# Early gathered steps beside the query product, and low weight halves on GpSimd in one stretch of a decoder-layer kernel

## The chip, the cores and the metric

The kernel runs on one core of a Trainium2 chip. The metric is the device time of one execution in microseconds (us), and less is better. The time of the kernel before is the median of three runs; beside them one execution was profiled, and every row shown here is of that one.

## The reference

The kernel computes one hybrid decoder layer on 512 tokens with 2048 channels, in float32:

```
x = x + concat[conv_group(xn), swa_group(xn)] @ w_out
x = x + peer(rms_norm(x))

peer: qh   = xt @ peer_w_q                    # 8 heads, two halves of 128
      sub  = qh . peer_sub_keys               # 128 scores per half
      v1, i1 = top_k(sub[0], 16); v2, i2 = top_k(sub[1], 16)
      cand = v1[:, None] + v2[None, :]        # best 16 of the sums
      experts = e1 * 128 + e2; gates = softmax(vals)
      h = xt . peer_u[experts];  a = gelu(h) * gates
      y = sum over 8 heads x 16 of a * peer_v[experts]
```

Each token thus picks 128 of 16384 experts, each one row of peer_u and one row of peer_v.

## The kernel before

The work goes in this order: the input product with convolution and attention, the two halves of the output product, the query product (`wq`) with the choice of experts, and then the experts themselves. All weights stream as **units** of 128x1024 float32 (512 KB). `stream` (L124 to L137) loads a unit into `w_raw` by SyncE's queue, ScalarE copies it rounded into `w_hi` (L135) and VectorE subtracts to get the rest, `w_lo` (L136); `w_hi` and `w_lo` have three buffers each, `w_raw` four from the second half of the output product on. Each product is three matmuls (high by high, low by high, high by low). Units 0 to 51 are the input product, 52 to 83 the output product, 84 to 115 the query product, and from 116 on come the experts.

The experts are computed in two ways. For the first 352 tokens they are **dense**: every expert is computed for every token. The sweep (`expert_tile`, L914) multiplies `peer_u`, the fold (`fold_group`, L960) multiplies `peer_v` by the gated results. One expert tile or one fold step is two units, 48 matmuls of 352 columns, and is called a **tick** here (`step`, L908): ticks 1 to 72 are sweep, 73 to 184 take turns of 8 sweep and 8 fold ticks, 185 to 256 are fold. The query product is 8 heads of 4 units, 24 matmuls of 512 columns each; after a head its queries go through `qhh` and `qhl` (L171, L172) into the score matmuls of `head_sub` (L676 to L678).

The other 160 tokens are **gathered**: `gather_step` (L829) fetches one row of `peer_u` or `peer_v` per partition by an indirect DMA that GpSimd issues (L821, 1 MB into `grow`, two buffers). VectorE then does one instruction over 128x2048: a product with its sum for `peer_u` (L837), a multiply and add into `yrow` for `peer_v` (L851). There are 320 steps: 128 + 32 over `un`, then 128 + 32 over `vn`. At the very end `yrow` goes through four products (`yo`, L1029), four copies (L1030) and one store (L1031).

When a gathered step is written into the program is set by the tick: from tick 11 (`START` = 10) to tick 247 (`END`) the steps are spread evenly, and the gather is put behind the first matmul of the tick (`add_manual_dep`, an order for the planner and no wait on the chip). The planner decides the order of each engine's queue beforehand; each engine then works through its queue in order.

```
if tick[0] > START:
    gather_until(int((tick[0] - START) * STEPS / (END - START)) + 1, first)
```

The choice of experts is VectorE work (`top16`, `gates`, `decode`) put into two waiting lists by `head_topk` (L760). `pump` hands some of it out after each unit, by written costs; its last piece for a head, `head_idx` (L755), writes 16 columns of `idx`, the list of rows to gather for that head.

Of the kernel before, what the change touches and what calls it, by code (L numbers as in the profile page):

```python
# [9 lines left out]
FT = mybir.dt.float32  # L10
FR = mybir.dt.float32r
# [3 lines left out]
OP = mybir.AluOpType  # L15
AX = mybir.AxisListType

T, D = 512, 2048
KC = D // 128
NT = T // 128  # L20
TD = 352
# [4 lines left out]
GT = 16  # L26
AHEAD = 9
START = 10
END = 247.0
PUMP = 5.4  # L30
CONV_K = 31
HD, NQ = 64, 16
NK, PH, TOPK = 128, 8, 16
# [26 lines left out]
def hymba_layer(ctx: ExitStack, tc: tile.TileContext, xT, pos, par, row, wi, wo, wq, sk, ut, un, vt, vn,  # L60
                out_t, out_r, dbg=None):
    nc = tc.nc
# [9 lines left out]
    dram = ctx.enter_context(tc.tile_pool(name="dram", bufs=1, space=bass.MemoryType.DRAM))  # L72
    mm = ctx.enter_context(tc.tile_pool(name="mm", bufs=4, space=PS))
# [7 lines left out]
    def later(cost, fn, *a, low=False):  # L81
        queues[low].append((cost, fn, a))
# [3 lines left out]
    def pump(us):  # L86
        credit[0] = min(credit[0] + us, us)
        for q in queues:
            while q and credit[0] > 0:
                cost, fn, a = q.popleft()  # L90
                fn(*a)
                credit[0] -= cost

    def drain(low=True):
        for q in queues[:1 + low]:
            while q:
                _, fn, a = q.popleft()
                fn(*a)
# [26 lines left out]
    def stream(upto):  # L125
        while nxt[0] < min(upto, len(specs)):
            i = nxt[0]
            nxt[0] += 1
            raw = raws[-1][0].tile([128, 1024], FT, name="w_raw", bufs=raws[-1][1])
            with tc.high_priority(offset=400 if i >= 4 else 0):  # L130
                nc.sync.dma_start(raw, specs[i])
            hi = ring.tile([128, 1024], FR, name="w_hi", bufs=3)
            lo = ring.tile([128, 1024], FR, name="w_lo", bufs=3)
            with tc.high_priority(offset=400):
                nc.scalar.activation(hi, raw, AF.Copy)  # L135
                nc.vector.tensor_tensor(lo, raw, hi.bitcast(FT), op=OP.subtract)  # L136
            units[i] = (hi, lo)  # L137

    def unit(ahead=1):
        i = nxt[1]  # L140
        nxt[1] += 1
        stream(i + 1 + ahead)
        return units.pop(i)
# [26 lines left out]
    def split(hi, lo, src):  # L170
        nc.scalar.activation(hi, src, AF.Copy)  # L171
        nc.vector.tensor_tensor(lo, src, hi.bitcast(FT), op=OP.subtract)  # L172
# [444 lines left out]
    nh = np_.tile([128, KC, T], FR, name="nh")  # L617
    nl = np_.tile([128, KC, T], FR, name="nl")
# [37 lines left out]
    es_q = ExitStack()  # L656
    wqp = es_q.enter_context(tc.tile_pool(name="wqp", bufs=1, side="right"))
# [10 lines left out]
    def head_sub(h, qh, ql, kh, kl):  # L668
        vv = kp.tile([128, NT, 2, 16], FT, name="vv", bufs=8)
        ii = kp.tile([128, NT, 2, 16], U32, name="ii", bufs=8)  # L670
        hs[h] = {"vv": vv, "ii": ii}
        hs[h]["sub"] = []
        st = kp.tile([128, 2, T], FT, name="subT", bufs=1)
        for p in range(2):
            ps = aux_bank([128, T], "subT")
            nc.tensor.matmul(ps, kh[:, p], qh[:, p], start=True, stop=False)  # L676
            nc.tensor.matmul(ps, kl[:, p], qh[:, p], start=False, stop=False)
            nc.tensor.matmul(ps, kh[:, p], ql[:, p], start=False, stop=True)  # L678
            nc.scalar.activation(st[:, p], ps, AF.Copy)
        for tp in range(2):  # L680
            ps = aux_bank([128, 2, 2, 128], "sub")
            for t in range(2):
                for p in range(2):
                    ts = slice((2 * tp + t) * 128, (2 * tp + t) * 128 + 128)
                    nc.tensor.transpose(ps[:, t, p], st[:, p, ts], ident)
            sub = kp.tile([128, 2, 2, 128], FT, name="sub", bufs=4)
            nc.scalar.activation(sub, ps, AF.Copy)
            hs[h]["sub"].append(sub)
# [66 lines left out]
    def head_idx(h):  # L755
        s = slice(h * 16, h * 16 + 16)
        nc.vector.scalar_tensor_tensor(idx[:, s], E1[:, 3, h], 128.0, E2[:, 3, h], op0=OP.mult, op1=OP.add)
        nc.vector.tensor_copy(GA3[:, s], GA[:, 3, h])

    def head_topk(h):  # L760
        for t in range(NT):
            later(2.1, first16, h, t)
        later(0.8, cands, h, low=True)
        for t in range(NT):
            later(1.0, second16, h, t, low=True)
        later(2.5, gates, h, low=True)
        later(3.3, decode, h, 0, low=True)
        later(3.3, decode, h, 1, low=True)
        later(0.2, head_idx, h, low=True)

    def lane_lists():
# [6 lines left out]
        for l in range(LANES):  # L778
            nc.scalar.dma_start(idxb[l * NB:l * NB + NB], ib[ps_, l * SB:l * SB + SB])
            nc.scalar.dma_start(GB3[l * NB:l * NB + NB], ga[:, l * SB:l * SB + SB])  # L780

    for h in range(PH):
        kr = wqp.tile([128, 2, 128], FT, name="kr", bufs=2)
        nc.sync.dma_start(kr, sk[h])
        kh = wqp.tile([128, 2, 128], FR, name="kh", bufs=2)
        kl = wqp.tile([128, 2, 128], FR, name="kl", bufs=2)
        split(kh, kl, kr)
        banks = [mm.tile([128, T], FT, name="mm") for _ in range(2)]
        for u in range(4):
            hi, lo = unit()  # L790
            for kc in range(4):
                k = 4 * u + kc
                for j in range(2):
                    s = slice(kc * 256 + j * 128, kc * 256 + j * 128 + 128)
                    nc.tensor.matmul(banks[j], hi[:, s], nh[:, k], start=k == 0, stop=False)  # L795
                    nc.tensor.matmul(banks[j], hi[:, s], nl[:, k], start=False, stop=False)  # L796
                    nc.tensor.matmul(banks[j], lo[:, s], nh[:, k], start=False, stop=k == KC - 1)  # L797
            pump(3.6)
        qh = wqp.tile([128, 2, T], FR, name="qhh", bufs=1)
        ql = wqp.tile([128, 2, T], FR, name="qhl", bufs=1)  # L800
        for j in range(2):
            split(qh[:, j], ql[:, j], banks[j])
        head_sub(h, qh, ql, kh, kl)
        head_topk(h)
    drain(low=False)
    es_q.close()

    later(0.5, lane_lists, low=True)
    H = [dram.tile([128, 4, TD], FT, name=f"H{i}") for i in range(32)]
    NCH = TD // GT  # L810
    G = dram.tile([16, 128, NCH, 8, GT], FT, name="G")

    pu = ctx.enter_context(tc.tile_pool(name="pu", bufs=1))
    h3 = gat.tile([128, 128 + SB], FT, name="h3")
# [1 line left out]
    STEPS = 2 * (128 + SB)  # L816
# [34 lines left out]
            nc.vector.scalar_tensor_tensor(y, g, h3[:, k:k + 1], y, op0=OP.mult, op1=OP.add)  # L851

    done = [0]

    def gather_until(n, after):
        while done[0] < min(n, STEPS):
            gather_step(done[0], after)
            done[0] += 1

    es_g = ExitStack()  # L860
    gpl = []
# [42 lines left out]
        later(3.4, dense_gates, q, low=True)  # L904

    tick = [0]

    def step(first, us):  # L908
        tick[0] += 1
        if tick[0] > START:  # L910
            gather_until(int((tick[0] - START) * STEPS / (END - START)) + 1, first)
        pump(us)

    def expert_tile(e, out):  # L914
# [173 lines left out]
```

## Time and profile before

| | us |
|---|---|
| median of 3 runs | 2887.02 |
| lowest and highest run | 2884.67 and 2904.49 |
| the profiled execution, whole | 2885.64 |
| its span, first to last instruction | 2883.9 |
| TensorE busy in it | 2817.3 |

Times in rows are from the span's start. The query product runs from 569 to 769, the ticks from 769 to 2852. A row of a group of instructions gives busy time and mean duration; a wait is put down to what was released last. Matmul durations overlap their neighbours, so that a matmul of 323 ns may come every 160 ns.

### The profile page before, as it was taken

To read this page: it belongs to the slowest core of one execution; us is meant where nothing else is said; L and a number is where in the kernel's file an instruction comes from. 1 tells how busy PE (TensorE), PEld (TensorE's weight loads), DVE (VectorE), ACT (ScalarE), POOL (GpSimd) and SP (SyncE) were. 2 spreads that over 40 slices of the span, in tenths; PEclk is the share of its full clock that TensorE was granted. 3 is DMA by queue.
4 is the path that set the end of the run, shared out by engine and by line. 5 is a ranking of instruction groups with operands and counts; after the bars stand their busy time and mean duration, and the time that the engine had idled before them with its cause. 6 is when DMAs were issued, how large, how long until landed. Compare 5 with 4: busy or idle time off the path is not lost.

```text
span 2883.9 us, 43602 instructions
## 1 busy us (share of the span) xinstructions
PE 2817.3 (98%) x16995; PEld 2693.7 (93%) x16995; DVE 2369.5 (82%) x3586; ACT 1209.1 (42%) x1879; POOL 468.8 (16%) x337
## 2 busy tenths in 40 slices
PE   8999999999999999999999999999999999999996
PEld 8998877788899999999999999999999999999995
DVE  7888996579998988787777778887888888888886
ACT  5666435343343886666323232333333333333321
POOL 0000000000002222221122122222222232112221
PEclk9999999999999999999999999999999999999998
DMA  5222322433259999999999899988898888888787
GB/s 174 74 70 77 110 96 90 148 98 115 94 179 329 334 356 326 336 337 341 345 341 336 307 320 346 348 317 332 324 350 329 342 334 342 325 339 330 299 335 245
DMA packets 203918, 761.90 MB, mean 264 GB/s; under 512 B 18560, under 2 KB 70912, under 8 KB 160384
## 3 DMA queue, kind: packets, MB, share of 16 engines
q1 hardware_dynamic: 103584, 378.66, 36.7%
q0 software_dynamic: 46080, 335.56, 30.8%
q10 hardware_dynamic: 54048, 44.90, 4.8%
q8 instruction: 133, 2.18, 0.3%
q14 instruction: 73, 0.60, 0.1%
HBM read 715.37 MB, written 43.65 MB: 263 GB/s over the span
## 4 chain that ended last, share of the span: by engine, by line
PE 65%; issue 19%; DMA 7%; POOL 5%; DVE 4%; ACT 1%; POOLq 0%; DVEq 0%; ACTq 0%
PE mm L974 9%; PE mm L973 9%; PE mm L971 9%; POOL grow L821 5%; PE mm L924 5%; PE mm L925 5%; PE mm L922 4%; DMA grow<-vn,idxb 3%; PE mm L581 2%; DMA grow<-vn,idx 2%; PE mm L582 2%; PE mm L796 2%; PE mm L795 2%; PE mm L797 2%; PE mm L494 2%
## 5 line engine op out<-in xcount | busy, mean ns | idle before, releaser
L135 ACT ACTIVATE w_hi<-w_raw 128x1024 fp32r<-128x1024 f32 x628 | 664.0, 1059 | 1237.5 <-PE mm L973 596.5
L136 DVE TENSOR_TENSOR w_lo<-w_raw,w_hi 128x1024 fp32r<-128x1024 f32 x628 | 768.7, 1229 | 189.5 <-ACT w_hi L135 185.9
L971 PE MATMUL mm<-ah,w_hi 128*128 128x352 f32 x2048 | 661.1, 324 | 11.4 <-DVE acc L981 11.4
L924 PE MATMUL mm<-nl,w_hi 128*128 128x352 f32 x2048 | 667.0, 326 | 0.0
L925 PE MATMUL mm<-nh,w_lo 128*128 128x352 f32 x2048 | 665.8, 326 | 0.6 <-DVE w_lo L136 0.5
L922 PE MATMUL mm<-nh,w_hi 128*128 128x352 f32 x2048 | 665.1, 325 | 0.0
L973 PE MATMUL mm<-al,w_hi 128*128 128x352 f32 x2048 | 663.0, 324 | 0.2 <-DVE al L172 0.2
L974 PE MATMUL mm<-ah,w_lo 128*128 128x352 f32 x2048 | 652.9, 324 | 8.9 <-DVE w_lo L136 8.8
L851 DVE SCALAR_TENSOR_TENSOR yrow<-grow,h,yrow 128x2048 f32<-128x2048 f32 x160 | 376.0, 2350 | 97.1 <-DMA grow<-vn,idx 63.2
L837 DVE SCALAR_TENSOR_TENSOR grow<-grow,xrow 128x2048 f32<-128x2048 f32 x160 | 366.1, 2288 | 73.6 <-DMA grow<-un,idx 58.0
L971 PEld LDWEIGHTS mm<-ah,w_hi 128*128 128x128 f32 x2048 | 386.3, 189 | 12.8 <-DVE acc L981 8.3
L974 PEld LDWEIGHTS mm<-ah,w_lo 128*128 128x128 f32 x2048 | 384.5, 189 | 12.6 <-DVE w_lo L136 12.6
L973 PEld LDWEIGHTS mm<-al,w_hi 128*128 128x128 f32 x2048 | 386.9, 189 | 0.5 <-DVE al L172 0.5
L925 PEld LDWEIGHTS mm<-nh,w_lo 128*128 128x128 f32 x2048 | 384.9, 188 | 1.8 <-DVE w_lo L136 1.7
L922 PEld LDWEIGHTS mm<-nh,w_hi 128*128 128x128 f32 x2048 | 384.9, 188 | 0.2
L924 PEld LDWEIGHTS mm<-nl,w_hi 128*128 128x128 f32 x2048 | 384.8, 188 | 0.1
L821 POOL DMA_INDIRECT grow<-un,idx x128 | 183.3, 1432 | 1097.4 <-DVE grow L837 774.6
L821 POOL DMA_INDIRECT grow<-vn,idx x128 | 194.2, 1517 | 631.6 <-DVE yrow L851 602.9
L289 DVE SCALAR_TENSOR_TENSOR mix_c<-h,par,mix_c 128x512 f32<-128x512 f32 x240 | 173.8, 749 | 1.6
L981 DVE TENSOR_TENSOR acc<-acc,mm 128x352 f32<-128x352 f32 x240 | 116.6, 519 | 41.8 <-PE mm L974 41.7
L890 ACT ACTIVATE og<-oh,kt 128x128 f32<-128x128 f32 x352 | 111.4, 391 | 28.2 <-DVE oh L887 23.0
L894 PE MATMUL gps<-og,oh 128*128 128x128 f32 x704 | 116.8, 274 | 0.0
(267 smaller groups left out, 3601.2 us busy)
## 6 DMA issues: line engine op xcount, KB each, us to landing
w_raw<-ut SPq DMA_DIRECT2D x256, 512.0 KB
w_raw<-vt SPq DMA_DIRECT2D x256, 512.0 KB
w_raw<-wi SPq DMA_DIRECT2D x52, 512.0 KB
G<-gt ACTq DMA_DIRECT2D x22, 1024.0 KB
Gb<-G SPq DMA_DIRECT2D x16, 1408.0 KB
w_raw<-wo SPq DMA_DIRECT2D x32, 512.0 KB
w_raw<-wq SPq DMA_DIRECT2D x32, 512.0 KB
H<-gl ACTq DMA_DIRECT2D x18, 704.0 KB
```

What stands on the lines that cost most here:

```text
L135: nc.scalar.activation(hi, raw, AF.Copy)
L136: nc.vector.tensor_tensor(lo, raw, hi.bitcast(FT), op=OP.subtract)
L289: nc.vector.scalar_tensor_tensor(mix_c[:, c], h[:, k:k + T], w, mix_c[:, c], op0=OP.mult, op1=OP.add)
L821: i = nc.gpsimd.indirect_dma_start(out=g, out_offset=None, in_=src, in_offset=bass.IndirectOffsetOnAxis(ap=at, axis=0))
L837: nc.vector.scalar_tensor_tensor(g, g, 1.0, rows["x"], op0=OP.mult, op1=OP.mult, accum_out=h3[:, k:k + 1])
L851: nc.vector.scalar_tensor_tensor(y, g, h3[:, k:k + 1], y, op0=OP.mult, op1=OP.add)
L922: m = nc.tensor.matmul(bank, hi[:, s], nh[:, k, :TD], start=k == 0, stop=False)
L924: nc.tensor.matmul(bank, hi[:, s], nl[:, k, :TD], start=False, stop=False)
L925: nc.tensor.matmul(bank, lo[:, s], nh[:, k, :TD], start=False, stop=k == KC - 1)
L971: m = nc.tensor.matmul(banks[j], hi[:, ws], ah[:, ee], start=ee == 0, stop=False)
L973: nc.tensor.matmul(banks[j], hi[:, ws], al[:, ee], start=False, stop=False)
L974: nc.tensor.matmul(banks[j], lo[:, ws], ah[:, ee], start=False, stop=ee == 7)
```

## The change

Four edits. The query loop moves below `gather_until`, and after the second and the fourth unit of each head one gathered step is written, if a list is ready: `head_idx` counts heads as their pieces are handed out, and 16 steps per head may be done. In ticks 1 to 10 there is one step per tick, and from tick 11 the steps still left are spread up to tick 240. Units 86 to 131 (from the third unit of the query product to the end of tick 8) have their `w_lo` computed by GpSimd. The pool `pu` with the two `grow` buffers is opened ahead of the query loop.

```diff
-END = 247.0
+END = 240.0
+POOL_LO = (86, 132)
...
-                nc.vector.tensor_tensor(lo, raw, hi.bitcast(FT), op=OP.subtract)
+                eng = nc.gpsimd if POOL_LO[0] <= i < POOL_LO[1] else nc.vector
+                eng.tensor_tensor(lo, raw, hi.bitcast(FT), op=OP.subtract)
...
     def head_idx(h):
...
+        heads[0] += 1
...
     def gather_until(n, after):
-        while done[0] < min(n, STEPS):
+        ready = STEPS if heads[0] == PH else 16 * heads[0]
+        while done[0] < min(n, ready):
             gather_step(done[0], after)
             done[0] += 1
...
     for h in range(PH):
         for u in range(4):
...
+            if u % 2 == 1:
+                gather_until(done[0] + 1, m)
             pump(3.6)
...
+    early = [0]
     def step(first, us):
         tick[0] += 1
-        if tick[0] > START:
-            gather_until(int((tick[0] - START) * STEPS / (END - START)) + 1, first)
+        if tick[0] <= START:
+            early[0] = done[0] + 1
+            gather_until(early[0], first)
+        else:
+            gather_until(early[0] + int((tick[0] - START) * (STEPS - early[0]) / (END - START)) + 1, first)
         pump(us)
```

## Rows read from the trace of the kernel before

**Rows 1.** The page, part 1: busy time, share of the span, instructions

```profile
PE 2817.3 (98%) x16995; PEld 2693.7 (93%) x16995; DVE 2369.5 (82%) x3586; ACT 1209.1 (42%) x1879; POOL 468.8 (16%) x337
```

**Rows 2.** Waits of PE: engine, line, releaser: total us, times, longest

```profile
PE yo L1029 <- DVE yrow L851: 21.6, 1, 21.6
PE mm L971 <- DVE acc L981: 11.4, 5, 4.3
PE mm L974 <- DVE w_lo L136: 8.8, 11, 2.8
```

**Rows 3.** The end: last fold matmuls of a line, then the timeline in order

```profile
L974 PE MATMUL mm<-ah,w_lo x2048: 317/323/624, 1466.4 to 2851.7; 128*128 128x352 f32 x187
...
2871.15 2.35 DVE L851 SCALAR_TENSOR_TENSOR yrow<-grow,h,yrow 128x2048 f32<-128x2048 f32 x1 [3.41 <-DMA grow<-vn,idxb]
2873.56 6.17 PE L1029 MATMUL yo<-yrow,fold_s 128*128 128x512 f32 x8 [21.58 <-DVE yrow L851]
...
2880.37 0.36 SPq L1031 DMA_DIRECT2D out_r<-grow  x1
```

**Rows 4.** Windows by stage: all engines' busy us (instructions), granted clock, DMA share, GB/s

```profile
569.00:769.00 200.00, 200.00 (x907) 162.28 (x907) 177.60 (x721) 75.62 (x113) 2.78 (x2) 0.99 0.30 98
769.00:845.00 76.00, 76.00 (x476) 75.65 (x475) 75.08 (x292) 35.42 (x44) 0.00 (x0) 1.00 0.46 153
...
1350.00:1850.00 500.00, 487.90 (x3018) 485.92 (x3017) 387.06 (x417) 165.34 (x208) 108.11 (x84) 0.99 0.90 331
...
2200.00:2700.00 500.00, 493.10 (x3050) 490.40 (x3050) 422.90 (x462) 161.81 (x200) 114.76 (x70) 1.00 0.89 336
2700.00:2850.00 150.00, 148.75 (x925) 148.17 (x924) 123.74 (x110) 41.90 (x45) 40.42 (x26) 1.00 0.83 310
```

**Rows 5.** Windows of line 851 alone, a gathered step over vn: VectorE busy (x steps)

```profile
2200.00:2700.00 500.00, 162.10 (x69) 1.00 0.89 336
2700.00:2850.00 150.00, 62.22 (x27) 1.00 0.83 310
2850.00:2884.00 34.00, 13.02 (x6) 0.62 0.50 175
```

**Rows 6.** Timeline of POOL and DVE where the first list and gathers come

```profile
676.37 0.27 DVE L757 SCALAR_TENSOR_TENSOR idx<-E,E 128x16 int32<-128x16 f32 x1
...
677.62 1.09 POOL L821 DMA_INDIRECT grow<-un,idx  x1 [291.56 <-DVE ii L666]
679.02 1.69 POOL L821 DMA_INDIRECT grow<-un,idx  x1 [0.30 <-issue]
855.09 0.93 POOL L821 DMA_INDIRECT grow<-un,idx  x1 [174.39 <-DVE grow L837]
```

**Rows 7.** Groups of instructions: x count, busy us, mean ns, idle before and releasers

```profile
L136 DVE TENSOR_TENSOR w_lo<-w_raw,w_hi 128x1024 fp32r<-128x1024 f32 x628 | 768.7, 1229 | 189.5 <-ACT w_hi L135 185.9 <-PE mm L925 2.6
...
L837 DVE SCALAR_TENSOR_TENSOR grow<-grow,xrow 128x2048 f32<-128x2048 f32 x160 | 366.1, 2288 | 73.6 <-DMA grow<-un,idx 58.0 <-DMA grow<-un,idxb 14.7 <-DMA xrow<-XB 0.7
L821 POOL DMA_INDIRECT grow<-un,idx x128 | 183.3, 1432 | 1097.4 <-DVE grow L837 774.6 <-DVE ii L666 291.6 <-DVE w_lo L136 7.0
...
L349 POOL MEMSET vl<- 128x1024 f32 x1 | 1.0, 953 | 0.0
```

**Rows 8.** Waits of SP's DMA queue and of POOL: total us, times, longest

```profile
SPq L131 <- DVE w_lo L136: 2114.8, 560, 19.3
...
POOL grow L821 <- DVE grow L837: 925.0, 153, 174.4
```

**Rows 9.** Timeline at a head's end: VectorE's qhl, then the matmul on it

```profile
700.80 0.82 DVE L172 TENSOR_TENSOR qhl<-mm,qhh 128x512 fp32r<-128x512 f32 x1
...
704.08 0.39 PE L678 MATMUL subT<-qhl,kh 128*128 128x512 f32 x1
```

**Rows 10.** Timeline of DVE in a fold group where TensorE stood

```profile
1615.70 2.29 DVE L837 SCALAR_TENSOR_TENSOR grow<-grow,xrow 128x2048 f32<-128x2048 f32 x1 [5.14 <-DMA grow<-un,idx]
...
1617.91 1.22 DVE L136 TENSOR_TENSOR w_lo<-w_raw,w_hi 128x1024 fp32r<-128x1024 f32 x1
1619.05 0.95 DVE L981 TENSOR_TENSOR acc<-acc,mm 128x352 f32<-128x352 f32 x2
```

More of the change, by code (lines that the diff above doesn't have):

```diff
@@ L780, in lane_lists @@
             nc.scalar.dma_start(GB3[l * NB:l * NB + NB], ga[:, l * SB:l * SB + SB])
[L782 to L811, printed above, removed]
     pu = ctx.enter_context(tc.tile_pool(name="pu", bufs=1))
@@ L853, in hymba_layer @@
     done = [0]
+    heads = [0]
     def gather_until(n, after):
-        while done[0] < min(n, STEPS):
+        ready = STEPS if heads[0] == PH else 16 * heads[0]
+        while done[0] < min(n, ready):
             gather_step(done[0], after)
             done[0] += 1
+    for h in range(PH):
+        kr = wqp.tile([128, 2, 128], FT, name="kr", bufs=2)
+        nc.sync.dma_start(kr, sk[h])
+        kh = wqp.tile([128, 2, 128], FR, name="kh", bufs=2)
+        kl = wqp.tile([128, 2, 128], FR, name="kl", bufs=2)
+        split(kh, kl, kr)
+        banks = [mm.tile([128, T], FT, name="mm") for _ in range(2)]
+        for u in range(4):
+            hi, lo = unit()
+            for kc in range(4):
+                k = 4 * u + kc
+                for j in range(2):
+                    s = slice(kc * 256 + j * 128, kc * 256 + j * 128 + 128)
+                    m = nc.tensor.matmul(banks[j], hi[:, s], nh[:, k], start=k == 0, stop=False)
+                    nc.tensor.matmul(banks[j], hi[:, s], nl[:, k], start=False, stop=False)
+                    nc.tensor.matmul(banks[j], lo[:, s], nh[:, k], start=False, stop=k == KC - 1)
+            if u % 2 == 1:
+                gather_until(done[0] + 1, m)
+            pump(3.6)
+        qh = wqp.tile([128, 2, T], FR, name="qhh", bufs=1)
+        ql = wqp.tile([128, 2, T], FR, name="qhl", bufs=1)
+        for j in range(2):
+            split(qh[:, j], ql[:, j], banks[j])
+        head_sub(h, qh, ql, kh, kl)
+        head_topk(h)
+    drain(low=False)
+    es_q.close()
+    later(0.5, lane_lists, low=True)
+    H = [dram.tile([128, 4, TD], FT, name=f"H{i}") for i in range(32)]
+    NCH = TD // GT
+    G = dram.tile([16, 128, NCH, 8, GT], FT, name="G")
     es_g = ExitStack()
```

## The prediction

> **What bounds the kernel now.** I read the page first. TensorE is busy 2817.3 of 2883.9 us [rows 1], so whatever the change does for VectorE or GpSimd can only count where TensorE stands, and 66.6 us is all that it stands. Next I read the waits of TensorE, to see where [rows 2]: the longest single wait is 21.6 us, once, for the last gathered step before the `yo` products; the others are a few us each, for `acc` and `w_lo`. The timeline of the end shows the same [rows 3]: the last fold matmul starts at 2851.7, but the last gathered step runs on VectorE at 2871.15, the `yo` products start at 2873.56, the store is issued at 2880.37 and the span ends at 2883.9. The gathered steps, not the dense product, end last. The windows by stage then say where the rest is lost [rows 4]: 12.1 us in 1350 to 1850 (500 less 487.9), 6.9 us in 2200 to 2700, none from 569 to 845. In that early stretch VectorE is full (75.08 of 76 us from 769 on) and GpSimd all but empty (2.78 of 200 us), and TensorE doesn't stand once.
>
> Why do the gathered steps end last, though the program places the last one in tick 247 of 256? A tick is 48 matmuls. From 2200 to 2700 there are 3050 matmuls, 63.5 ticks [rows 4], and 69 steps [rows 5], 1.09 per tick, where the program wants 320 / 237 = 1.35. After 2200 come 69 + 27 + 6 = 102 steps, so 218 are done by then. Tick 256 ends at 2852 and a tick is some 7.8 us there, so 2200 is near tick 173, where the plan asks for 163 x 1.35 + 1 = 221: up to here the steps are on plan, and the last 72 ticks lose them. There the DMAs are 0.89 busy at 336 GB/s.
>
> **The change, part by part.** *Early steps.* I followed the waiting lists of `pump` with their written costs: the first head's list is handed out in the third unit of the fourth head, so the first early step stands after that head's fourth unit, and two follow per head: 1 + 2 x 4 = 9 in the query product. Ticks 1 to 10 add ten. 19 steps are thus placed by tick 10, and 301 are left for 230 ticks, 1.309 per tick in place of 1.35. The list isn't late: in the kernel before the first list is written at 676.37 and GpSimd issues two gathers at once, at 677.62 and 679.02, and then waits 174 us because the VectorE step that frees the first buffer stands at tick 11 in its queue [rows 6]. The change moves that step up; the pool opened earlier is first written by these gathers, 100 us after its opening, and costs nothing. Each early step costs GpSimd 1.43 us and VectorE 2.29 + 0.08 us [rows 7], together 19 x 2.37 = 45 us of VectorE between some 670 and 850. Their 19 MB meet DMAs that are 0.30 and 0.46 busy [rows 4].
>
> *Low halves on GpSimd.* 46 units leave VectorE, 46 x 1.23 = 57 us [rows 7], a little more than the early steps bring; VectorE's sum is 12 us smaller. What such an instruction takes on GpSimd no row shows. The nearest is a memset of the same size, 0.953 us [rows 7], which has no operand; with two operands to read I take twice that, 1.9 us, and as the ends 0.95 and three passes, 2.86 us. A query unit lasts 200 / 32 = 6.25 us and a tick about 7.65 us 476 matmuls in 76 us, [rows 4]. GpSimd then has at most 2 x 1.9 + 1.43 = 5.2 us of work in a tick, and 7.2 us at the upper end, so it keeps up at either and costs nothing, hidden behind TensorE's 48 matmuls of a tick, as long as nothing in its queue waits; without that cover each us over 7.65 would cost eight ticks one us each. The Trainium skill (GPSIMD Engine Reference, Performance versus the Vector engine) has 4497 ns for such an instruction over 2048 elements, by which half of it would be an estimated 2.25 us and a tick 5.9 us; no run here shows it yet. The loads behind it, on SyncE's queue, now wait for GpSimd in place of VectorE [rows 8], by at most 2.86 - 1.23 = 1.6 us later; four buffers hold three units of work ahead, 11 us in the sweep, so nothing there. Behind a `w_lo` on GpSimd stand the next gather and the next `w_lo`; for them waits TensorE, by up to two units.
>
> TensorE stood nowhere between 569 and 845, so none of this can make that stretch shorter; it can only make it longer. I put it at zero.
>
> *The end.* By the old plan's lag of 3 steps, tick 173 now finds 19 + 163 x 1.309 + 1 - 3 = 230 steps done, 90 left. At the old 69 steps up to 2700, 21 are left then, and at the rate of 2700 to 2850 (27 in 150 us, 5.6 us each) they are done at some 2820; at the slower rate of 1.09 per tick (7.25 us each) at 2852. In both cases the last fold ends no earlier than they do. The 21.6 us wait goes [rows 2]. What is late next is TensorE's own end: 2852.0, then `yo`, copies and store as before, 2883.9 - 2873.56 = 10.3 us, which gives 2862.3. If the planner sets `yo` ahead of the last fold matmuls, up to 6 us of that goes as well; before, lines further down in the program mostly stay behind, so I leave it in.
>
> *Thinner steps in the fold.* Where TensorE stood near 1620, VectorE had waited 5.14 us for a gather, with a `w_lo` and an `acc` queued behind it [rows 10]. With 1.309 in place of 1.35 steps per tick a step has 5.84 in place of 5.67 us, 3% more. The bounds are 0 and all 19.0 us of the two stretches; since 3% is little beside waits of 2 to 5 us, I take 3 us.
>
> Sum: the span 2883.9 - 21.6 - 3 = 2859.3. The profiled execution was 1.7 us over its span, so 2861; it lies 1.4 us under the median of 2887.02, so this is a gain of 25 to 26 us, 0.9%. A measurement of this kernel can tell about 1%, here 29 us: bounds 2858 and 2916.
>
> **The rivals.** *VectorE is held up by GpSimd (slower side).* If an instruction of VectorE with two operands can't run while GpSimd reads, then each of the 46 low halves may stop VectorE for its length: 46 x 1.9 = 87 us, less the 12 us saved, is 75 us more VectorE work. The idle time of VectorE from 569 to 769 is 22.4 us [rows 4], the rest, 53 us, reaches TensorE: `qhl` runs only 2.5 us ahead of the matmul that needs it [rows 9], and gathers and low halves stand behind VectorE's steps. Then 2861 + 53 = 2914. It decides from 26 us on, that is where each low half costs VectorE more than some 1.3 us. For it: VectorE has no slack from 769 on [rows 4]. Against: much of its work there is search over one operand, and one stop per low half needs it to meet one at once. The Trainium skill says just this (SBUF — State Buffer, Who interferes with whom): a VectorE instruction with two SBUF inputs contends with a GpSimd instruction that reads SBUF, the later one waiting for the earlier. By that rule the change moves work between two engines that share a read port, and gains no VectorE time; no row of the trace before has GpSimd reading beside VectorE, so it is open here. Chance 0.20.
>
> *A gather blocks GpSimd's queue.* With two buffers a gather waits for the VectorE step two before it, and the low halves behind it wait too. In the kernel before gathers over un waited 925.0 us for that step in 153 times [rows 8]; without the longest, 174.4, that is 4.9 us each. Ten ticks with 4.9 us, less 8 x 2.4 us that GpSimd has to spare, are 30 us: 2891, no change. Against it: at one step per tick the buffer is freed a tick earlier. Chance 0.10.
>
> *More goes than I count.* The `yo` products slip ahead (6 us) and half to most of the 19 us of fold stalls goes (9 to 15 us): 2861 + 3 - 18 = 2846. For it: VectorE's queue order is set anew, and gathers lead by more. Against: a load of gates and the accumulator also stand in those stretches. Chance 0.23.
>
> *It doesn't do what it says.* The lists come later than their written costs, the early steps wait, and the tail stays in part: 2875. Rows 6 speak against it. Chance 0.03.
>
> **How the numbers follow.** The forecast has 0.44, with a range of its own of 2850 to 2872. Faster by over 1%: all but a little of the 0.23, and 0.18 of the forecast's 0.44, 0.40. Slower by over 1%: half of the 0.20 and a little, 0.11. Within 1%: 0.49. The range reaches to 2840 and 2903 and leaves out a tenth on either side.
>
> **What would show it.** Right: the wait of `yo` for `yrow` gone, the last gathered step before the last fold matmul, 769 still the start of the sweep, and 46 `w_lo` rows on POOL of 1 to 3 us. Wrong: waits of TensorE for `w_lo` or `qhl` between 569 and 845; VectorE instructions with two operands longer or later there than before; POOL idle on `grow` with `w_lo` behind it. A last step still after the last fold would refute the sum of the end.

## The result, and the profile after

The median after is 2904.26 us (20 runs, 2898.85 to 2919.04) against 2887.11 before (20 runs): the ratio is 1.006, with an interval of 1.005 to 1.007. The kernel is slower, by 0.6%. The profiled execution took 2899.16 us, its span is 2897.4 us.

The page of the kernel after, part 1, as [rows 1]:

```profile
PE 2825.3 (98%) x16995; PEld 2700.4 (93%) x16995; DVE 2378.2 (82%) x3540; ACT 1209.7 (42%) x1877; POOL 575.9 (20%) x383
```

But for GpSimd's the shares are those of before. VectorE's sum says more: 46 instructions have left it (3540 after 3586), 57 us by [rows 7], and yet its busy time has risen, from 2369.5 [rows 1] to 2378.2. The waits of TensorE show where that hurts (line waited at, releaser, us in total, times, longest), as [rows 2]:

```profile
PE subT L680 <- DVE qhl L174: 19.2, 6, 5.8
...
PE mm L982 <- DVE acc L992: 6.5, 3, 3.0
...
PE mm L985 <- DVE w_lo L138: 5.3, 7, 2.8
...
PE mm L936 <- DVE w_lo L138: 3.8, 1, 3.8
PE mm L936 <- POOL w_lo L138: 3.5, 3, 3.1
```

The wait of `yo` for the last gathered step is gone. In its place stands a wait that didn't exist before: the score matmul of a head waits for `qhl` of VectorE, 19.2 us in six times. The end of the kernel after, the last matmuls of the fold and then the timeline, as [rows 3]:

```profile
L985 PE MATMUL mm<-ah,w_lo x2048: 317/323/495, 1519.0 to 2889.5; 128*128 128x352 f32 x187
...
L823 DVE SCALAR_TENSOR_TENSOR yrow<-grow,h,yrow x160: 2343/2348/2362, 1820.8 to 2843.8; 128x2048 f32<-128x2048 f32 x160
...
2889.64 3.59 PE L1040 MATMUL yo<-yrow,fold_s 128*128 128x512 f32 x8
```

The last gathered step starts at 2843.8, 46 us before the last fold matmul, and `yo` follows the last fold matmul at once. From there to the end are 7.9 us; before they were 32.2. So the tail gave what was forecast, and the rest took more than that back. The windows by stage, as [rows 4]:

```profile
569.00:769.00 200.00, 186.75 (x831) 149.46 (x830) 177.87 (x621) 71.96 (x109) 88.19 (x35) 0.98 0.34 116
769.00:845.00 76.00, 66.83 (x351) 61.62 (x351) 76.00 (x252) 22.18 (x28) 39.32 (x20) 0.91 0.52 187
...
1350.00:1850.00 500.00, 493.07 (x3096) 491.54 (x3095) 388.43 (x403) 182.19 (x246) 103.46 (x83) 1.00 0.91 337
...
2200.00:2700.00 500.00, 495.13 (x3072) 493.70 (x3071) 417.82 (x447) 163.34 (x200) 107.97 (x70) 1.00 0.89 333
```

Where TensorE stood nowhere before, it now stands 13.2 us of 200 and 9.2 us of 76, while VectorE is full; the fold stages are a little better than before (493.07 after 487.90, 495.13 after 493.10). Boundaries read from the first or last matmul of a product put the whole difference of 13.5 us in place:

| stage | before | after | difference |
|---|---|---|---|
| up to the query product | 568.8 | 571.6 | +2.8 |
| query product | 200.3 | 224.6 | +24.3 |
| ticks 1 to 176 (to the last sweep tile) | 1453.7 | 1468.8 | +15.1 |
| fold alone | 628.9 | 624.5 | -4.4 |
| after the last fold matmul | 32.2 | 7.9 | -24.3 |

What fills VectorE between 569 and 900 is seen in its groups of instructions there (count, busy us, mean ns, idle before; `dec_oh` is written by `decode`, in the choice of experts):

```profile
L809 DVE SCALAR_TENSOR_TENSOR grow<-grow,xrow 128x2048 f32<-128x2048 f32 x19 | 64.7, 3405 | 0.0
L753 DVE TENSOR_TENSOR dec_oh<-dec_oh,iif 128x1024 f32<-128x1024 f32 x12 | 21.1, 1760 | 0.0
```

A gathered step takes 3405 ns on average, where it took 2288 before [rows 7]. Ten of the 19 take 2.27 to 2.33 us, the other nine 3.65 to 6.79. One timeline each of GpSimd and VectorE shows why (start, duration), the longest of them first:

```profile
860.87 4.73 POOL L138 TENSOR_TENSOR w_lo<-w_raw,w_hi 128x1024 fp32r<-128x1024 f32 x2
...
860.96 6.79 DVE L809 SCALAR_TENSOR_TENSOR grow<-grow,xrow 128x2048 f32<-128x2048 f32 x1
...
714.06 6.75 POOL L138 TENSOR_TENSOR w_lo<-w_raw,w_hi 128x1024 fp32r<-128x1024 f32 x2 [9.72 <-ACT w_hi L136]
...
714.80 3.80 DVE L809 SCALAR_TENSOR_TENSOR grow<-grow,xrow 128x2048 f32<-128x2048 f32 x1
...
718.66 2.30 DVE L736 CAST dec_f<-dec_i 128x256 f32<-128x256 uint32 x1
...
721.38 0.67 DVE L174 TENSOR_TENSOR qhl<-mm,qhh 128x512 fp32r<-128x512 f32 x1
...
722.10 0.50 PE L680 MATMUL subT<-qhl,kh 128*128 128x512 f32 x1 [2.93 <-DVE qhl L174]
```

At 860.87 GpSimd begins two low halves in a row; the step that starts 0.09 us later ends 2.2 us after both, as if it had run only then. At 714 the step takes 1.5 us and a conversion 2.0 us more than usual (368 ns is the mean of that conversion before) while two low halves run, `qhl` stands behind them in VectorE's queue, and TensorE waits 2.93 us for it.

### The profile page after: what moved, and what is told of

It is laid out like the page before. It is cut to its first block, busy times and chain, and to the rows that moved or that the text cites. A ratio compares the mean times of both kernels' runs of the same rounds, so it can differ in the third digit from the quotient of the medians.

```text
span 2897.4 us, 43597 instructions
## 1 busy us (share of the span) xinstructions
PE 2825.3 (98%) x16995; PEld 2700.4 (93%) x16995; DVE 2378.2 (82%) x3540; ACT 1209.7 (42%) x1877; POOL 575.9 (20%) x383
## 4 chain that ended last, share of the span: by engine, by line
PE 62%; issue 20%; DVE 10%; POOL 5%; DMA 2%; ACT 1%; POOLq 0%; DVEq 0%; ACTq 0%
PE mm L985 10%; PE mm L984 10%; PE mm L982 10%; POOL grow L793 5%; PE mm L935 4%; PE mm L933 4%; PE mm L936 4%; PE mm L583 2%; PE mm L496 2%; PE mm L495 2%; PE mm L494 2%; PE mm L584 2%; DVE grow L809 2%; PE mm L582 2%; PE mm L312 1%
## 5 line engine op out<-in xcount | busy, mean ns | idle before, releaser
L138 DVE TENSOR_TENSOR w_lo<-w_raw,w_hi 128x1024 fp32r<-128x1024 f32 x582 | 709.9, 1224 | 221.9 <-ACT w_hi L136 219.5
L809 DVE SCALAR_TENSOR_TENSOR grow<-grow,xrow 128x2048 f32<-128x2048 f32 x160 | 387.1, 2421 | 61.2 <-DMA grow<-un,idx 41.4
L793 POOL DMA_INDIRECT grow<-vn,idx x128 | 177.3, 1385 | 644.0 <-DVE yrow L823 603.2
L138 POOL TENSOR_TENSOR w_lo<-w_raw,w_hi 128x1024 fp32r<-128x1024 f32 x46 | 125.4, 2733 | 315.3 <-ACT w_hi L136 290.2
```

Of the source, the lines that this page charges most:

```text
L138: eng.tensor_tensor(lo, raw, hi.bitcast(FT), op=OP.subtract)
L793: i = nc.gpsimd.indirect_dma_start(out=g, out_offset=None, in_=src, in_offset=bass.IndirectOffsetOnAxis(ap=at, axis=0))
L809: nc.vector.scalar_tensor_tensor(g, g, 1.0, rows["x"], op0=OP.mult, op1=OP.mult, accum_out=h3[:, k:k + 1])
```

## The experiments

Two theories of the loss: the low halves on GpSimd stop VectorE's instructions, which is the first rival of the prediction; or VectorE was overfilled by the early steps, wherever the low halves run. For the gain: the early lead, or the thinner steps that follow from it.

### Which part loses: each part alone

The change without GpSimd:

```diff
-POOL_LO = (86, 132)
+POOL_LO = (0, 0)
```

> The changed kernel with all low halves back on VectorE (POOL_LO empty); early steps and the end at tick 240 stay. Theory A (GpSimd's reads stop VectorE's instructions with two operands): the gathered product over 128x2048 is back from 3405 to 2290 ns on average, GpSimd has no low half, and the sweep, which began at 796.0 us with the change and at 768.9 before, begins at 770 to 785, since VectorE still has 45 us of early steps to fit in. The end keeps its 24 us, total 2860 to 2875, faster than before. Theory B (the early steps alone overload VectorE, which was full): VectorE now has 57 us more than in the changed kernel, the sweep begins later than 796, and the total is 2905 or more.

Measured: 2849.34 us, ratio to before 0.9863 [0.9837, 0.9889]. Its group of gathered steps from 569 to 900, its window from 769 on, and the lines of the end:

```profile
L809 DVE SCALAR_TENSOR_TENSOR grow<-grow,xrow 128x2048 f32<-128x2048 f32 x28 | 63.9, 2282 | 0.8 <-DMA grow<-un,idx 0.8
```

```profile
769.00:900.00 131.00, 131.00 (x816) 130.32 (x816) 131.00 (x329) 51.81 (x65) 24.64 (x19) 1.00 0.81 295
```

```profile
L985 PE MATMUL mm<-ah,w_lo x2048: 317/323/495, 1469.0 to 2839.6; 128*128 128x352 f32 x187
...
L823 DVE SCALAR_TENSOR_TENSOR yrow<-grow,h,yrow x160: 2337/2345/2354, 1772.1 to 2793.9; 128x2048 f32<-128x2048 f32 x160
```

VectorE is full here too (131.00 of 131), with nine steps more done by 900 than after, and TensorE doesn't stand at all from 569 to 900. So an overfilled VectorE isn't the cause, and the early steps with their `END` are worth 1.4% by themselves, 11 us more than the first theory expected at best (2860). The spans differ by 2897.4 - 2847.5 = 49.9 us: 23.7 in the query product, 24.8 in ticks 1 to 176.

The other part alone, the kernel before with low halves on GpSimd and no early step:

```diff
+POOL_LO = (86, 132)
...
-                nc.vector.tensor_tensor(lo, raw, hi.bitcast(FT), op=OP.subtract)
+                eng = nc.gpsimd if POOL_LO[0] <= i < POOL_LO[1] else nc.vector
+                eng.tensor_tensor(lo, raw, hi.bitcast(FT), op=OP.subtract)
```

> The kernel before with units 86 to 131 on GpSimd and nothing else. Theory A: 46 instructions of some 2.4 us on GpSimd stop the decode and split instructions of VectorE; VectorE is relieved of 57 us and loses a part of it again, TensorE waits a little, the sweep begins at 770 to 785, and since the gathered steps still end last the total is 2885 to 2905. Theory B (only the early steps cost): VectorE is relieved by 57 us, the sweep begins at 769 as before, total 2880 to 2888.

Measured: 2925.18 us, 1.013 [1.0099, 1.0161]. The waits of TensorE and one group of VectorE from 569 to 900:

```profile
PE subT L680 <- DVE qhl L174: 14.7, 6, 7.0
...
PE yo L1031 <- DVE yrow L853: 14.4, 1, 14.4
```

```profile
L753 DVE TENSOR_TENSOR dec_oh<-dec_oh,iif 128x1024 f32<-128x1024 f32 x16 | 29.7, 1859 | 0.1
```

The sweep starts at 795.4, as late as after, without any early step: it isn't the gathered steps that have to be stopped. The same instruction took 1321 ns before and takes 1859 here. The loss is larger than was expected (2905 at most); VectorE is no longer full (112.72 us of 131 from 769 on) and TensorE still stands. Nor does it take gathers in GpSimd's queue: GpSimd issues the first one at 873.7 here, after its last low half, and ticks 1 to 176 still take 1471.8 us, 18.1 more than before. The two parts don't add up: -1.4% and +1.3% alone, +0.6% together.

### Is it what GpSimd reads?

Three kernels with the change and another instruction in place of GpSimd's subtraction. First one that only writes (`w_lo` of the 46 units is zero, so that part of the two products is left out):

```diff
-                eng = nc.gpsimd if POOL_LO[0] <= i < POOL_LO[1] else nc.vector
-                eng.tensor_tensor(lo, raw, hi.bitcast(FT), op=OP.subtract)
+                if POOL_LO[0] <= i < POOL_LO[1]:
+                    nc.gpsimd.memset(lo.bitcast(FT), 0.0)
+                else:
+                    nc.vector.tensor_tensor(lo, raw, hi.bitcast(FT), op=OP.subtract)
```

> The changed kernel with the 46 instructions of GpSimd replaced by a memset of the same tile: the low halves of these units are left out (zero), and GpSimd writes but doesn't read. Theory A in its narrow form (it is GpSimd's reading that stops VectorE): the gathered product is at 2290 ns, TensorE doesn't wait for qhl, the sweep begins at 769 to 772, total near 2862. If it is GpSimd's occupation of the port in any form, or the early steps themselves, the product stays near 3400 ns or the sweep begins near 790.

Measured: 2855.91 us (one run). Groups of GpSimd (whole span) and VectorE (569 to 900), and a step of VectorE with a memset that runs inside it:

```profile
L138 POOL MEMSET w_lo<- 128x1024 f32 x46 | 44.4, 966 | 366.9 <-DVE x L563 172.3 <-PE mm L851 165.9 <-PE mm L938 28.7
...
L811 DVE SCALAR_TENSOR_TENSOR grow<-grow,xrow 128x2048 f32<-128x2048 f32 x27 | 61.6, 2281 | 4.9 <-DMA grow<-un,idx 4.9
...
810.34 2.28 DVE L811 SCALAR_TENSOR_TENSOR grow<-grow,xrow 128x2048 f32<-128x2048 f32 x1
810.81 0.96 POOL L138 MEMSET w_lo<- 128x1024 f32 x1 [1.79 <-PE mm L938]
```

Not one step is stretched, no wait for `qhl` is left, and the sweep starts at 769.3. GpSimd's queue, its order with the gathers and its writing cost the query product nothing. The span is 6.6 us over that with the low halves on VectorE, and that falls into the ticks; it is one run, and runs of the change itself spread over 20 us. VectorE's busy time shows the difference without that scatter (the page, part 1, with all low halves on VectorE and then with the memsets):

```profile
PE 2811.4 (99%) x16995; PEld 2692.5 (95%) x16995; DVE 2368.2 (83%) x3586; ACT 1214.0 (43%) x1881; POOL 457.9 (16%) x337
PE 2812.5 (99%) x16995; PEld 2693.5 (94%) x16995; DVE 2321.8 (81%) x3540; ACT 1209.6 (42%) x1877; POOL 504.3 (18%) x383
```

Without the 46 low halves VectorE is busy 46 us less. In the change, with the same 3540 instructions, it is busy 2378.2 us: GpSimd's subtractions lengthen VectorE's other work by 56 us.

Then one that reads one operand, the raw weights (the subtraction is left out, so `w_lo` isn't the low half):

```diff
+                if POOL_LO[0] <= i < POOL_LO[1]:
+                    nc.gpsimd.tensor_copy(lo, raw)
```

> The changed kernel with the 46 instructions of GpSimd replaced by a copy of the raw tile into the low half: one operand is read in place of two, the subtraction is left out. If any read of GpSimd stops VectorE's instructions with two operands for its length, and such a copy takes some 1 to 1.3 us in place of 2.4, the gathered product averages 2.5 to 2.9 us in the early stretch, between 2.29 and 3.41, and the sweep begins at 770 to 785. If it takes two operands on GpSimd's side, the product stays at 2.29 and the sweep begins at 769 to 771.

Measured: 2864.37 us (one run). The mean step is 2347 ns: 22 of 25 are unstretched, three take 2.52 to 3.47. The copy is short, 1.04 us alone, and here GpSimd is the one that waits (timelines of GpSimd and VectorE):

```profile
816.02 1.04 POOL L138 CAST w_lo<-w_raw 128x1024 fp32r<-128x1024 f32 x1
819.41 3.07 POOL L138 CAST w_lo<-w_raw 128x1024 fp32r<-128x1024 f32 x1 [2.35 <-issue]
...
819.32 2.27 DVE L811 SCALAR_TENSOR_TENSOR grow<-grow,xrow 128x2048 f32<-128x2048 f32 x1
```

The step began 0.09 us earlier and takes its usual time; the copy lasts 2 us longer. So the stop goes both ways. Here the one that began second waits; but at 801.54 a step takes 3.47 us beside a copy that begins only at 801.80 and takes its 1.05, so the starts in the profile don't always tell who waits. Both the sweep's start (769.9) and the mean step lie under what stops by a copy were expected to make, and the three stretched steps speak against the other expectation: a short read stops VectorE, but seldom.

Last, the same subtraction in four pieces:

```diff
+                if POOL_LO[0] <= i < POOL_LO[1]:
+                    for c in range(4):
+                        s = slice(256 * c, 256 * c + 256)
+                        nc.gpsimd.tensor_tensor(lo[:, s], raw[:, s], hi[:, s].bitcast(FT), op=OP.subtract)
```

> The changed kernel with each low half on GpSimd cut into four instructions of 128x256. If the two engines take turns by instruction, VectorE waits for some 0.65 us at a time in place of 2.4: the gathered product averages 2.5 to 2.9 us, the sweep begins at 772 to 785, total 2865 to 2885. If GpSimd keeps the read port over instructions that follow each other without a gap (the 6.79 us product of the changed kernel lay beside two low halves in a row), the cuts change nothing for VectorE and lengthen GpSimd's work by some 46 x 3 x 0.1 us: sweep at 796 or later, total 2900 to 2915.

Measured: 2883.86 us, 0.9982 [0.9968, 0.9995]. The group of VectorE and the timeline of GpSimd:

```profile
L813 DVE SCALAR_TENSOR_TENSOR grow<-grow,xrow 128x2048 f32<-128x2048 f32 x22 | 54.2, 2463 | 4.8 <-DMA grow<-un,idx 4.8
```

```profile
600.45 2.83 POOL L140 TENSOR_TENSOR w_lo<-w_raw,w_hi 128x256 fp32r<-128x256 f32 x4 [3.21 <-ACT w_hi L136]
```

The same bytes on the same engine, here in 2.83 us in place of 2.34 to 2.40; over all 46 units GpSimd is busy 3.8 us for one, since now it waits more. No step takes longer than 2.86 us (0.57 over), the sweep starts at 780.0, and 20 us of the 55 between the medians of the change with and without GpSimd come back. Time and sweep are what taking turns was expected to give, at a mean step just under it (2463 ns). So the length of one stop decides about a third of the loss.

### Where it is lost

GpSimd only from the first tick on (16 units):

```diff
-POOL_LO = (86, 132)
+POOL_LO = (116, 132)
```

> The changed kernel with GpSimd's low halves in ticks 1 to 8 alone (16 of the 46), the query product's on VectorE. With GpSimd's reads as the cause, the query product is undisturbed, the sweep begins at 769 to 772, and some of the 25 us that the changed kernel lost after that (sweep and fold ticks up to 176 took 1469 us there, 1444 with all low halves on VectorE) stay: total 2862 to 2875. If the low halves hurt only beside the queries' qhl, nothing is lost in the ticks: 2847 to 2853.

Measured: 2875.83 us, 0.9971 [0.9958, 0.9984], a little above what was expected. The sweep starts at 770.5, so the query product's 24 us are those of the 30 units in it. Ticks 1 to 176 take 1468.9 us, as in the change itself. The waits of TensorE, and groups of GpSimd and VectorE from 769 to 900:

```profile
PE mm L936 <- POOL w_lo L138: 7.7, 4, 3.0
```

```profile
L138 POOL TENSOR_TENSOR w_lo<-w_raw,w_hi 128x1024 fp32r<-128x1024 f32 x14 | 38.8, 2787 | 17.1 <-ACT w_hi L136 14.4 <-PE mm L935 2.7
...
L809 DVE SCALAR_TENSOR_TENSOR grow<-grow,xrow 128x2048 f32<-128x2048 f32 x15 | 34.8, 2321 | 1.5 <-DMA grow<-un,idx 1.5
```

The steps are hardly stretched here (2321 ns), but other instructions of VectorE are. The longest, with the two low halves beside it:

```profile
801.27 4.76 POOL L138 TENSOR_TENSOR w_lo<-w_raw,w_hi 128x1024 fp32r<-128x1024 f32 x2
...
802.08 5.04 DVE L751 TENSOR_TENSOR dec_oh<-iof,dec_f 128x1024 f32<-128x1024 f32 x1
```

Of 131 us from 769 on TensorE stands 15.3: 7.7 for GpSimd's low halves, 4.3 for VectorE's and 3.2 for `w_hi`. So in the ticks low halves of GpSimd come late, and VectorE is stopped as well; which of the two counts for more, these runs don't separate. What the loss goes with is seen beside each other for the five kernels with early steps. "Longer" adds up VectorE's instructions from 560 to 900 that take over 0.3 us more than the median of the same instruction with all low halves on VectorE; the last column is the span over that kernel's 2847.5 us.

| GpSimd does, for 46 units | VectorE's instructions longer, us (count) | GpSimd for one unit, us | span longer, us |
|---|---|---|---|
| a memset | 4.3 (7) | 0.97 | 6.6 |
| a copy | 13.0 (15) | 1.25 | 15.1 |
| the subtraction, but for 16 units alone | 27.2 (14) | 2.74 | 25.8 |
| the subtraction in quarters | 27.8 (52) | 3.8 | 34.1 |
| the subtraction (the change) | 58.6 (34) | 2.73 | 49.9 |

In these five the loss grows with how much VectorE is held up. It doesn't follow the time that GpSimd takes for a low half: the quarters take it longest and lose a third less than the change.

### Where the gain comes from

The kernel before with the last step placed earlier or later (`END` is 247 in it; 240 makes 1.39 steps per tick, 256 makes 1.30):

```diff
-END = 247.0
+END = 240.0
```

> The kernel before with END at 240 in place of 247 and nothing else: 1.39 steps per tick. My reading of the end (in the fold ticks only 1.09 steps per tick get through, whatever the plan) says that the steps reach tick 173 with 7 more done and so end some 40 us earlier at best, near the last fold matmul: total 2865 to 2885. The rival, that the DMAs are full and a thicker plan only puts more waits on VectorE in the sweep, says 2885 to 2900.

```diff
-END = 247.0
+END = 256.0
```

> The kernel before with END at 256: 1.30 steps per tick without any lead. If the pace counts, the last fold matmul starts 8 to 15 us before the 2851.7 of the kernel before, at 2837 to 2844; the gathered steps have no lead and end last, some 10 to 25 us later than the 2871 of before, so the total is 2885 to 2910. If the lead counts, the last fold matmul is at 2848 to 2856 and the total is 2890 to 2915.

Measured: with 240 2884.56 us, 0.9988 [0.9969, 1.0007]; with 256 2901.65, 1.0058 [1.0038, 1.0078]. From the kernel with 256, the last fold line and the wait at the end:

```profile
L974 PE MATMUL mm<-ah,w_lo x2048: 317/323/498, 1467.7 to 2838.9; 128*128 128x352 f32 x187
```

```profile
PE yo L1029 <- DVE yrow L851: 51.6, 1, 51.6
```

Moving `END` alone shifts time between two places: at 240 the wait of `yo` is 15.4 us, but the last fold matmul comes at 2854.3; at 256 it comes at 2838.9, 12.8 us earlier than before [rows 3], and `yo` waits 51.6. With 240 the last step starts at 2867.5, only 3.7 us earlier than before where I had up to 40, and the total lies on the edge between the two expectations. With 256 the last fold matmul is where the pace was expected to put it. By these two the stalls in the fold go with the pace and the tail with the lead, so that only steps done before tick 10 can improve both.

The change without GpSimd and without the nine steps in the query loop, then with them and other ends:

```diff
-            if u % 2 == 1:
-                gather_until(done[0] + 1, m)
```

> Low halves on VectorE, one step in each of ticks 1 to 10, but none in the query product: 10 or 11 steps by tick 10, then some 1.35 per tick up to tick 240. If the lead of 19 steps is what frees the end, 9 steps less mean 9 x 5.6 = 50 us later, and the last step, which ran at 2794 with low halves on VectorE, comes at some 2844, level with the last fold matmul: total 2849 to 2860. If the even thinner plan in the sweep is what counts, TensorE stands more in the first fold groups: 2860 to 2875.

> Low halves on VectorE, early steps as in the change, but END at 247: 1.27 steps per tick. The last step ran 46 us before the last fold matmul with END at 240; at 247 it has some 30 us less, so the end still hangs on TensorE. Waits on gathers in the fold groups get fewer: total 2842 to 2852, at best 7 us under the 2849 of END at 240. The rival: the steps end last again, 2855 to 2870.

> Low halves on VectorE, 19 early steps, END at 233: the lead of the change with the pace of the kernel before, 301 / 223 = 1.35 steps per tick. If the pace is what makes TensorE stand in the fold groups between 1350 and 2200 us, it stands there again by 12 to 25 us more than at 1.31: last fold matmul at 2850 to 2865, total 2858 to 2873. If the lead is what counts, the last fold matmul stays at 2838 to 2842 and the total at 2847 to 2852.

| low halves on VectorE | steps per tick | median us | ratio to before | last fold matmul | TensorE busy, 1350 to 2200 |
|---|---|---|---|---|---|
| ten early steps, `END` 240 | 1.35 | 2873.16 | 0.9941 [0.991, 0.9973] | 2865.1 | 827.72 |
| 19 early steps, `END` 233 | 1.35 | 2865.19 | 0.993 [0.991, 0.9949] | 2857.9 | 833.28 |
| 19 early steps, `END` 240 | 1.31 | 2849.34 | 0.9863 [0.9837, 0.9889] | 2839.6 | 843.44 |
| 19 early steps, `END` 247 | 1.27 | 2847.72 | 0.9855 [0.9831, 0.988] | 2838.2 | 844.66 |

In none of the four does `yo` wait for a step. In the first the last step starts at 2825.5, 40 us before the last fold matmul: it had lead enough, and still loses 24 us, so the first expectation for it (2849 to 2860) fails. The second and the fourth lie where the pace was expected to put them. Its wait of TensorE, and the window from 1350 of the second and the third:

```profile
PE mm L980 <- DVE acc L990: 17.6, 7, 4.8
```

```profile
1350.00:2200.00 850.00, 833.28 (x5175) 828.27 (x5174) 667.39 (x638) 294.23 (x390) 199.14 (x141) 0.99 0.88 327
```

```profile
1350.00:2200.00 850.00, 843.44 (x5288) 842.00 (x5287) 679.76 (x650) 302.76 (x396) 183.44 (x142) 1.00 0.90 332
```

With one more step in 25 ticks TensorE gets through 113 fewer matmuls in the same 850 us. Below 1.31 per tick nothing more is gained: the last two rows can't be told apart. Both beat the kernel before and the change; they are the best versions found. Over all kernels with low halves on VectorE, TensorE is busy 827.7 to 837.5 us from 1350 to 2200 with 1.35 steps per tick and more, and 841.6 to 844.7 with 1.31 and less. Within each group the order doesn't follow the pace (1.39 is at 835.1), and `END` also moves where the planner puts every step; that the pace itself is the cause is likely and not shown.

Last, a step after every unit of the query product (27 steps by tick 10, `END` 247, 1.24 per tick):

```diff
-            if u % 2 == 1:
-                gather_until(done[0] + 1, m)
+            gather_until(done[0] + 1, m)
```

> Low halves on VectorE, END at 247, and an early step after every unit of the query product in place of every second: 27 steps by tick 10, then 293 / 237 = 1.24 per tick. If VectorE's full queue there is free for TensorE as long as no low half is late, the sweep still begins at 769 to 772 and the fold groups gain a little again: total 2838 to 2848. If VectorE's 19 us more there are one load too many, the sweep begins at 775 or later: 2850 to 2860.

Measured: 2860.21 us, 0.9914 [0.9894, 0.9933], 12.5 us more than with a step every second unit. The query product takes it without loss (sweep at 767.8), but then:

```profile
769.00:900.00 131.00, 127.71 (x789) 125.51 (x788) 129.28 (x330) 50.66 (x64) 28.72 (x20) 1.00 0.83 303
```

TensorE stands 3.3 us there, and the last fold matmul comes at 2849.4, 11 us later than with `END` 247 and 19 steps. Of the rest, some 5 us lie in the fold after the last sweep tile. In all fold ticks together TensorE waits 15.3 us for `acc` and `w_lo`, where it waited 9.2 with 19 steps, though the pace is thinner still. Neither expectation holds whole: the product was not delayed, the total was. Why the fold stands more here stays open.

## Why the prediction was wrong

**The step that failed is the low halves on GpSimd: "so it keeps up at either and costs nothing", and for the stretch from 569 to 845 "I put it at zero".** It cost 49.9 us of the span. I had asked whether GpSimd keeps up, and it does: its 46 low halves take 125 us in some 310. I had not asked what VectorE does meanwhile, except in a rival. What decides is that the work moved isn't work removed: while GpSimd reads, VectorE's instructions with two operands stand, and some conversions and copies too. In 34 instructions that comes to 58.6 us, as much as the 57 us that were to leave VectorE. The source of GpSimd's line (min/median/max) has the price of one:

```profile
L138 POOL TENSOR_TENSOR w_lo<-w_raw,w_hi x46: 2343/2402/5697, 559.9 to 869.0; 128x1024 fp32r<-128x1024 f32 x46
```

2.34 us alone, over my 1.9 and inside its ends. The estimate of 2.25 us by the Trainium skill (GPSIMD Engine Reference, Performance versus the Vector engine) was nearer than mine.

**The first rival is what happened.** It put the loss at 53 us and the time at 2914; the loss is 49.9, the time 2904, just beyond the upper end of the range. That the two losses lie so near is luck: it has one stop of 1.9 us per low half, 87 us, where the trace has 34 stops of 1.7 us on average, and it adds the loss to 2861, where the run without GpSimd took 2849. The 19 steps lose 19 x (3405 - 2288) = 21 us, the rest is in `dec_oh`, conversions and other short instructions; in the ticks low halves come late besides. Its sign "for it" was the right one to weigh: VectorE had no slack from 769 on [rows 4], and `qhl` ran 2.5 us ahead of its matmul [rows 9], little more than one low half takes. My reason against it, that one stop per low half must meet a two-operand instruction at once, was right in the count (34 stops for 46 low halves) and too weak to set the cost at zero: nine of 19 steps were stopped, one of them by two low halves in a row.

The rule of the Trainium skill (SBUF — State Buffer, Who interferes with whom) that a VectorE instruction with two SBUF inputs contends with a GpSimd instruction that reads SBUF, and not with one that only writes it, is what these traces show: 3405 ns beside the subtraction, 2281 beside the memset. The copy that waits 2 us behind a step agrees with its statement that the order of issue decides who waits; the step at 801.54, which waits for a copy that starts 0.26 us after it, doesn't by the starts in the profile.

**Early steps at no cost: right.** 19 steps by tick 10, VectorE full, and TensorE stood nowhere from 569 to 900 in the run without GpSimd. The lists came in time (the first early step starts at 684.9 there), so the last rival falls. The 57 us that were to leave VectorE weren't needed at all.

**The end: right, a little better than counted.** The last step starts at 2793.9 without GpSimd, before the 2820 I had; after the last fold matmul 7.9 us remain, not 10.3, since `yo` takes 3.59 us and not 6.17. Before, TensorE had stood 21.6 us ahead of it, and the granted clock of the last 34 us was 0.62 [rows 3, 5].

**Thinner steps: right in kind, a term mis-sized.** I took 3 us of bounds 0 to 19. Without GpSimd the last fold matmul comes at 2839.6 after 2851.7: 12.1 us. The stalls don't fall in proportion to the pace: 3% fewer steps per tick took most of them away.

So the sum should have read, on the span: 2859.3 - 9.1 (fold) - 2.7 (end, 24.3 for 21.6) = 2847.5 without GpSimd, which is what that run shows, and + 49.9 = 2897.4 with it. These terms are taken from the runs, so that they fit is bookkeeping and no test. **The other rivals:** more goes than I count (2846) has nearly the time of the run without GpSimd, 2849; of its two terms the fold's holds (12.1 of 9 to 15), but the `yo` products start after the last fold matmul there too. A gather that blocks GpSimd's queue has no support in the query product, where the memset stood in the same queue at no cost. In the ticks its sign shows: before the gather at 812.23 GpSimd stands 8.05 us, with a low half right behind it. But TensorE waits only 3.5 us in all for GpSimd's low halves in the change, and the kernel before with low halves on GpSimd loses 18.1 us in the ticks without a gather in GpSimd's queue before 873.7. So the loss doesn't need it; what it adds wasn't separated.

## What to carry to other kernels

Before work is moved to an idle engine, ask whether the two engines can run at once: here GpSimd's two-operand work beside a full VectorE cost some 1.1 us of the kernel per instruction (49.9 / 46), and VectorE's busy time didn't fall. Test each half of a combined change alone: one half here is worth -1.4%, the other +1.3%. When work is spread over a long loop, try several paces: here the stalls were fewer at 1.31 steps per tick and less than at 1.35 and more, and starting earlier gave both the slower pace and the lead at the end.

## What the runs showed of the hardware

- A VectorE instruction that starts just after one of GpSimd can wait through two of GpSimd's in a row: 6.79 us for one of 2.27. In pieces of 128x256 on GpSimd no step waited over 0.57 us.
- Not only two-operand instructions were stopped: a conversion of 128x256 took 2.30 us, where its mean was 368 ns before. Such short ones wait beside the memset too: the same conversion took 1.01 us at 702.57, with a memset from 702.47 to 703.42, while no gathered step and no `dec_oh` did.
- A stall can cost TensorE more than its length. After 3.36 us of standing the matmuls come every 0.29 us in place of 0.16 for 6 us (timeline of TensorE after, and a window in it with a granted clock of 0.50, the 1.2 GHz level):

```profile
806.77 0.80 PE L680 MATMUL subT<-qhl,kh 128*128 128x512 f32 x1 [3.36 <-DVE qhl L174]
...
808.24 0.50 PE L936 MATMUL mm<-nh,w_lo 128*128 128x352 f32 x1
808.54 0.50 PE L933 MATMUL mm<-nh,w_hi 128*128 128x352 f32 x1
...
813.20 0.33 PE L933 MATMUL mm<-nh,w_hi 128*128 128x352 f32 x1
813.36 0.32 PE L935 MATMUL mm<-nl,w_hi 128*128 128x352 f32 x1
```

```profile
808.00:812.00 4.00, 4.00 (x15) 3.91 (x14) 4.00 (x8) 2.12 (x4) 0.00 (x0) 0.50 0.01 4
...
769.00:900.00 131.00, 111.91 (x596) 104.67 (x596) 131.00 (x414) 41.70 (x53) 61.03 (x31) 0.90 0.59 209
```

From 569 to 900 TensorE stands 13.2 + 19.1 = 32.3 us, and the granted clock is 0.90 over the last 131 us. Counted in steps of half a us where TensorE is busy, the lower clock takes 10 us there and 4 from 569 to 769, where the run without GpSimd has 0 and 2: by this estimate about a quarter of the 49.9 us.
